# Hybrid retention and RG-LRU layer on one core: half of the retention heads two places later, transpositions four places behind, gate weights loaded a step ahead, S2 in tiles of its own

## The chip, the core and the metric

One core of a Trainium2 chip. The metric is the time of one execution on the device, in microseconds (us). The engines of the core run side by side, each through its own instructions in a fixed order, and wait for each other by semaphores: TensorE (PE, with its weight loads as PEld), VectorE (DVE), ScalarE (ACT), GpSimd (POOL, nearly unused here) and SyncE (SP), which issues nearly all the transfers (DMAs) here.

## What is computed

One decoder layer on 1024 tokens of width 1024: a normalisation, one wide input projection, two token mixers side by side, one output projection with the residual, a final normalisation.

```python
xn = rms_norm(h, norm_in_g)
q, k, v, g_ret, x_lru, g_lru = jnp.split(xn @ w_in, IN_SPLITS, axis=-1)
o_ret = group_norm_heads(chunkwise_retention(rotary(q), rotary(k) * d ** -0.5, v))
y_ret = o_ret * silu(g_ret)                       # 8 heads of 128, chunks of 128 tokens
xc = causal_depthwise_conv(x_lru, conv_w, conv_b)
y_lru = rg_lru(xc, gate_a_w, ..., lru_lambda) * silu(g_lru)   # gates: 8 blocks of 128 x 128
h = h + concat(y_ret, y_lru) @ w_out
return rms_norm(h, norm_out_g)
```

Retention goes chunk by chunk: the scores of a chunk with a decay mask, times v, plus q times a state that each chunk updates; then a group norm per head and the gate.

## The kernel before

All matmuls of the projections are fp32 by three matmuls of rounded parts: `mm3` (L109 to L113; the matmul itself is L112) multiplies high by high, high by low and low by high. `split` (L104 to L107) makes the two parts of an operand: the cast to the high part on ACT (L106), the rest on DVE (L107). Large products are done as seven block products P1 to P7 in place of eight, with sums and differences of blocks as operands (`combine`, L188, on DVE).

The program goes through these stages; the times are those of the profiled execution.
- `v_phase` (6 to 88 us): the projection to v, by P1, P2, P5, P6, P7, P3, P4 in this order. The left operand of P6 is the block difference S2. Its DVE combines and its casts stand in the code behind S1's and S3's, and S2 is written in place over the tiles of block A11 (named xA). `token_rms` loads x once more (tile xt), squares it on ACT (L201) and so gets the row scale, which a matmul with the identity spreads over the partitions (`make_rstd_b`, L219).
- 12 quads XL, GL and G, three for each of four pairs p of LRU blocks (88 to 377 us). `Runner.step` runs the seven products of a quad, with the preparation of the next quad's weights (tile wraw) between them; at each `fill()` one entry of the list `fillers` runs. The quad's `post` appends what remains to that list. For XL this is the convolution (tiles cx, cy, xc; its parts xh and xlo), the gate weights (`gate_w_parts`: load of tile graw and its split into gw), the gates (`lru_gates`: 12 matmuls of xh and xlo by gw for each of two blocks), decay and scan.
- 8 quads for q and k (377 to 500 us): rotation on DVE, then writes to `qk_d` in DRAM, from which the retention loads q and k again.
- the LRU half of the output projection (500 to 663 us): 16 units of 24 matmuls (tiles wo, yt), with the pieces of `Retention` as fillers in between. `Retention(0)` (called a) takes four heads, `Retention(1)` (b) the other four. For each chunk n there are `scores(n)` (L796, and L803 for the transposed k; it also loads chunk n+1's q and k, tile qkc, and v), `state(n)` (L817), `out(n)` (L834, L835, and the group norm into tile yn, L848) and `flip(n)` (four 128 x 128 transposes of yn on PE, L856, times the gate, then a write to `o_d`). A piece is a place in the list, and the units of the projection run some 12 matmuls from one place to the next.
- the retention half of the output projection by seven products (663 to 739 us) and the final normalisation.

Which instruction goes where on an engine is decided by a scheduler from the program's order and its dependencies; within an engine the order is then fixed. SP's queue too is in order: a DMA whose tile is still in use holds up those behind it. Tiles come from pools with a fixed number of buffers (vb 6, vo 10, w4 10, and so on); `big()` takes one of the ten buffers of w4.

Of the kernel before, what the change touches and what calls it, by code (L numbers as in the profile page):

```python
# [16 lines left out]
P = 128  # L17
# [23 lines left out]
def hybrid_layer(  # L41
# [25 lines left out]
    def pool_on(side, name, bufs):  # L67
        return tc.tile_pool(name=name, bufs=bufs, side=side, reuse_waits="tile")
# [117 lines left out]
    def combine(out, a, b, op):  # L186
        for o, x_, y_ in zip(out, a, b):
            dve.tensor_tensor(out=o, in0=x_, in1=y_, op=op)  # L188
# [58 lines left out]


    def v_phase():
        with pool_on("left", "vb", 6) as vb, pool_on("left", "vo", 10) as vo:  # L250
            bw, c, todo = {}, {}, []

            def half():
# [13 lines left out]
            def w_parts(name, src):  # L267
                bw[name] = Parts(slabs)
                for i in range(2):
                    bw[name].put(i, src[i])  # L270
# [60 lines left out]

            combine(b11, b11, b22, ALU.add)
            w_parts("P6", b11)
            s3 = xr["A21"]
            combine(s3, xr["A11"], s3, ALU.subtract)
            s2 = xr["A11"]
            combine(s2, s1, s2, ALU.subtract)
            x_parts("P6", s2)
            sp.dma_start(out=cst_sb, in_=cst)
            sp.dma_start(out=ident, in_=ident_in)  # L340
            todo.extend(token_rms(vb, "bt"))
# [279 lines left out]
    def lru_quads():  # L621
        quads = []
        for p in range(4):
            bs = (2 * p, 2 * p + 1)
            g, gw = {}, []

            def gate_w_parts(p=p, gw=gw):
                gr = sums.tile([P, 2, 512], F32, name="graw", tag="sum")
                sp.dma_start(out=gr[:, 0], in_=gate_w[:, 512 * p:512 * p + 512])
                gw.append(gwp.tile([P, 2, 512], F32R, name="gw", tag="gw"))  # L630
                split(gr[:, 0], gw[0][:, 0], gw[0][:, 1])

            def post_x(q, bs=bs, gw=gw, gate_w_parts=gate_w_parts):
                x0, x1 = lru_conv(bs[0], q.cx), lru_conv(bs[1], q.cy)
                fillers.extend(x0 + [
                    gate_w_parts, x1[0], lambda: lru_gates(gw[0], bs[0]), *x1[1:], None, None,
                    lambda: lru_gates(gw[0], bs[1]), lambda: lru_decay(bs), lambda: lru_root(bs), lambda: lru_scan(bs[0]),
                    lambda: lru_scan(bs[1])])

            def post_g(q, bs=bs, g=g):  # L640
                def gate(b, c):
                    dve.tensor_tensor(out=c, in0=c, in1=rstd_b, op=ALU.mult)
                    act.activation(out=c, in_=c, func=AF.Silu)
                    g[b] = c
                for b, c in zip(bs, (q.cx, q.cy)):
                    fillers.extend([lambda b=b, c=c: gate(b, c), lambda b=b: lru_gated(b, g)])

            quads.append(Quad(C_XL + 256 * p, w4, "w4", post_x))
            quads.append(Quad(C_GL + 256 * p, w4, "w4", post_g))
            quads.append(Quad(C_G + 256 * p, w4, "w4", post_gr(p)))  # L650
        return quads
# [120 lines left out]
    class Retention:  # L772
        def __init__(self, hf):
            self.hf = hf
            self.mask = mask_sb[:, 4 * hf:4 * hf + 4]
            self.st = None
            self.sm, self.qk, self.v, self.kn, self.g = {}, {}, {}, {}, {}

        def load(self, n):
            self.qk[n] = op["qkc"].tile([P, 2, 512], F32, name="qkc", tag="qkc")  # L780
            sp.dma_start(out=self.qk[n],
                         in_=qk_d[self.hf, n].rearrange("p j h c -> p j (h c)"))
            self.v[n] = ph_next["vc"].tile([P, 512], F32, name="vc", tag="vc")
            sp.dma_start(out=self.v[n], in_=v_d[self.hf, n])
            act.activation(out=self.v[n], in_=self.v[n], func=AF.Copy, scale=rstd[:, n:n + 1])
            self.g[n] = ph_next["gch"].tile([P, 512], F32, name="gch", tag="gch")
            sp.dma_start(out=self.g[n], in_=g_d[self.hf, n].rearrange("p h c -> p (h c)"))

        def scores(self, n):
            if n == 0:  # L790
# [35 lines left out]

        def out(self, n):

            hf, q, vn, sm, st = self.hf, self.qk.pop(n)[:, 0], self.v.pop(n), self.sm.pop(n), self.st
            po = psum()  # L830
            for h in range(4):
                hs = slice(h * P, (h + 1) * P)
                if st is not None:
                    pe.matmul(po[:, hs], q[:, hs], st[:, h], start=True, stop=False)  # L834
                pe.matmul(po[:, hs], sm[:, h], vn[:, hs], start=st is None, stop=True)  # L835
            stats = small.tile([P, 4, 6], F32, name="stats", tag="stats")
            mv = small.tile([P, 4, 2], F32, name="mv", tag="mv")
            heads(lambda h, hs: dve.bn_stats(out=stats[:, h], in_=po[:, hs]))
            heads(lambda h, hs: dve.bn_aggr(out=mv[:, h], in_=stats[:, h]))
            ve = small.tile([P, 4], F32, name="ve", tag="ve")  # L840
            dve.tensor_tensor(out=ve, in0=mv[:, :, 1], in1=cst_sb[:, H + 4 * hf:H + 4 * hf + 4],
                              op=ALU.add)
            rs = rsqrt_act(ve, 4)
            yn = ph_next["yn"].tile([P, 512], F32, name="yn", tag="yn")
            nb = small.tile([P, 4], F32, name="nb", tag="nb")
            dve.scalar_tensor_tensor(out=nb, in0=mv[:, :, 0], scalar=-1.0, in1=rs, op0=ALU.mult,  # L846
                                     op1=ALU.mult)
            heads(lambda h, hs: act.activation(out=yn[:, hs], in_=po[:, hs], func=AF.Identity,  # L848
                                               scale=rs[:, h:h + 1], bias=nb[:, h:h + 1]))
            self.yn = yn  # L850
            self.st = self.st_next

        def flip(self, n):

            py, yn = psum(), self.yn
            heads(lambda h, hs: pe.transpose(py[:, hs], yn[:, hs], ident))  # L856
            ot = ph_next["ot"].tile([P, 512], F32, name="ot", tag="ot")
            dve.tensor_tensor(out=ot, in0=py, in1=self.g.pop(n), op=ALU.mult)
            sp.dma_start(out=o_d[self.hf, :, :, n * P:(n + 1) * P].rearrange("h p c -> p h c"),
                         in_=ot.rearrange("p (h c) -> p h c", h=4))  # L860

    def pieces(a, b):

        def first(r, n):
            if n < NT:
                r.scores(n)
            if n:
                r.flip(n - 1)

        f = []  # L870
        for n in range(NT + 1):
            m = n - 1
            f.append(lambda n=n: first(a, n))
            if m >= 0:
                f.append(lambda m=m: first(b, m))
            if n < NT:
                f.append(lambda n=n: (a.state(n), a.out(n)))
            if m >= 0:
                f.append(lambda m=m: (b.state(m), b.out(m)))
        return f + [None, lambda: first(b, NT)]  # L880

    p_a, p_b, *rest = pieces(Retention(0), Retention(1))
    rest[0], rest[1] = rest[1], rest[0]
    fillers.extend([None, None, p_a, None, p_b] + rest)

    wt, ys, xop = {}, {}, {}

# [37 lines left out]
    for dh in range(2):  # L925
        cols = slice(dh * HALF, (dh + 1) * HALF)
        w_cur = w_o
        for t in range(NT):
            if dh == 0 and 0 < t < NT - 1:
                load_yl(t + 1)  # L930
            if dh == 0 and t == 2:
                w_o = group(D, HALF, (0,))
            ps = psum()
            unit_o(ps, yl[t], w_cur, slice(0, HALF), (3, 7) if dh == 0 else (2, 5, 7))
            r = hres[t][:, cols]
            with tc.issue_after(last_load[0].ins):
                sp.dma_start(out=r, in_=x[t * P:(t + 1) * P, cols])
            dve.tensor_tensor(out=r, in0=ps, in1=r, op=ALU.add)
            if dh == 0 and t == NT - 2:
                w_o += group(D, HALF, (2, 4, 6))  # L940
            if dh == 1 and t == 2:
                w_load("11", "wraw", 0, 0)
                w_parts("P1", "11")
            if dh == 1 and t == 4:
                w_load("21", "wraw", 1, 0)
                w_parts("P2", "21")
            if dh == 1 and t == 5:
                y_block(0, 0)
                y_parts("P1", ys[0, 0])
            if dh == 1 and t == 6:  # L950
                y_block(1, 0)
                w_load("11", "wraw", 0, 0)
# [196 lines left out]
```

## Time and profile before

| | |
|---|---|
| median of three runs | 748.6 us (748.37 to 748.61) |
| the profiled execution | 748.8 us |
| its span, first to last instruction | 747.0 us |
| PE busy | 724.4 us, 97% |
| DVE busy | 582.7 us, 78% |
| ACT busy | 425.5 us, 57% |
| mean granted clock of TensorE | 0.993 |

The profiled execution's time is 1.8 us longer than its span. PE is the busiest engine by far, so time is to be sought in the stretches where PE stands still or runs at a lower clock; the busy shares of the other engines are means over stages with different limits.

### The profile page before, as it was taken

What the parts mean: (1) busy time and instruction counts of PE and PEld (TensorE: products, weight loads), DVE (VectorE), ACT (ScalarE), POOL (GpSimd) and SP (SyncE); (2) the same over time, 40 slices, a digit from 0 to 9 for tenths busy, and PEclk for the clock granted to TensorE, in tenths of its full rate; (3) what the DMA queues carried; (4) which work ended last, traced back from release to release, by engine and by line L of the source; (5) the groups of instructions that cost most, each with busy time, mean ns of one, the idle gap of its engine ahead of it and who ended that gap; (6) DMA issues with size and microseconds to landing.
All of it is one profiled execution on the core that took longest, in us unless ns stands there. A gap on an engine that the chain in (4) does not pass through costs nothing.

```text
span 747.0 us, 9358 instructions
## 1 busy us (share of the span) xinstructions
PE 724.4 (97%) x3448; PEld 601.7 (81%) x3448; DVE 582.7 (78%) x960; ACT 425.5 (57%) x649; POOL 0.2 (0%) x4
## 2 busy tenths in 40 slices
PE   6999999999999999999999999997999999999995
PEld 5877888887788788878788888886989988888884
DVE  6899647678977977996799988686467565779996
ACT  6795435695689679669833333244444445424545
POOL 0000000000000000000000000000000000000000
PEclk9999999999999999999999999999899999999998
DMA  9862712122213410421644444569897776272006
GB/s 308 279 207 86 254 56 72 57 84 85 70 57 105 135 57 32 142 97 54 197 126 128 114 113 113 141 187 286 273 312 255 253 210 211 72 228 81 1 0 226
DMA packets 93806, 107.68 MB, mean 144 GB/s; under 512 B 4928, under 2 KB 66752, under 8 KB 93760
## 3 DMA queue, kind: packets, MB, share of 16 engines
q1 hardware_dynamic: 93616, 106.82, 45.5%
q8 instruction: 27, 0.44, 0.2%
q10 hardware_dynamic: 144, 0.26, 0.1%
q14 instruction: 19, 0.16, 0.1%
HBM read 77.71 MB, written 29.36 MB: 143 GB/s over the span
## 4 chain that ended last, share of the span: by engine, by line
PE 55%; DVE 22%; ACT 11%; DMA 7%; issue 4%; SPq 0%; DVEq 0%; ACTq 0%
PE pp L112 47%; DVE xc L561 2%; DVE h L1003 2%; PE pp L796 2%; PE pp L835 2%; PE pp L834 2%; DVE wt L107 2%; PE pp L817 1%; DVE wq L107 1%; DVE y L614 1%; PE pp L856 1%; ACT wq L106 1%; DVE blk L188 1%; DMA rot<-in_rot_t 1%; DMA blk<-o_d 1%
## 5 line engine op out<-in xcount | busy, mean ns | idle before, releaser
L112 PE MATMUL pp<-wh,wq 128*128 128x512 f32 x960 | 301.5, 390 | 1.6 <-DVE cy L471 0.7
L112 PEld LDWEIGHTS pp<-wh,wq 128*128 128x128 f32 x960 | 179.9, 188 | 42.5 <-ACT cy L461 2.3
L112 PE MATMUL pp<-wl,wq 128*128 128x512 f32 x480 | 186.9, 389 | 0.0
L112 PEld LDWEIGHTS pp<-wl,wq 128*128 128x128 f32 x480 | 90.1, 188 | 18.6
L112 PE MATMUL pp<-wo,yt 128*128 128x512 f32 x384 | 98.4, 403 | 0.0
L112 PEld LDWEIGHTS pp<-wo,yt 128*128 128x128 f32 x384 | 70.7, 191 | 13.1
L107 DVE TENSOR_TENSOR wq<-t,wq 128x1024 fp32r<-128x1024 f32 x40 | 48.6, 1220 | 38.6 <-ACT wq L106 31.5
L106 ACT CAST wq<-t 128x1024 fp32r<-128x1024 f32 x40 | 41.7, 1051 | 31.7 <-PE pp L112 22.0
L112 PE MATMUL pp<-wh,w 128*128 128x512 f32 x160 | 52.9, 391 | 0.1
L112 PE MATMUL pp<-wh 128*128 128x512 f32 x112 | 45.5, 406 | 6.9 <-ACT wh L106 6.9
L112 PE MATMUL pp<-wl,wh 128*128 128x512 f32 x112 | 44.6, 400 | 0.0
L112 PE MATMUL pp<-wh,wl 128*128 128x512 f32 x112 | 44.2, 399 | 0.0
L112 PEld LDWEIGHTS pp<-wh,w 128*128 128x128 f32 x160 | 30.0, 188 | 6.9 <-DVE w L107 0.6
L461 ACT COPY cy<-pp 128x512 f32<-128x512 f32 x20 | 11.6, 581 | 41.9 <-PE pp L112 41.3
L848 ACT ACTIVATE yn<-pp,nb,rs_y 128x128 f32<-128x128 f32 x64 | 24.1, 457 | 17.2 <-DVE nb L846 17.2
L112 PEld LDWEIGHTS pp<-wh 128*128 128x128 f32 x112 | 21.7, 194 | 12.1 <-ACT wh L106 7.3
L112 PE MATMUL pp<-wl,w 128*128 128x512 f32 x80 | 31.1, 389 | 0.0
L112 PE MATMUL pp<-wt,ylh 128*128 128x512 f32 x96 | 29.6, 389 | 0.0
L112 PE MATMUL pp<-wt,qkch 128*128 128x512 f32 x96 | 29.6, 389 | 0.0
L422 ACT CAST wq<-wraw 128x512 fp32r<-128x512 f32 x40 | 22.9, 617 | 9.0 <-PE pp L112 8.2
L106 ACT CAST wt<-blk 128x1024 fp32r<-128x1024 f32 x14 | 14.6, 1050 | 21.5 <-PE pp L112 18.0
L424 DVE TENSOR_TENSOR wq<-wraw,wq 128x512 fp32r<-128x512 f32 x40 | 26.8, 681 | 0.1
(179 smaller groups left out, 1303.7 us busy)
## 6 DMA issues: line engine op xcount, KB each, us to landing
wraw<-in_w_in SPq DMA_DIRECT2D x40, 512.0 KB, 4.8
qkc<-qk_d SPq DMA_DIRECT2D x16, 512.0 KB, 6.3
blk<-in_w_out SPq DMA_DIRECT2D x12, 512.0 KB, 5.5
bt<-in_w_in SPq DMA_DIRECT2D x20, 256.0 KB, 5.4
xA<-in_xT SPq DMA_DIRECT2D x16, 256.0 KB, 5.4
v_d<-vo SPq DMA_DIRECT2D x16, 256.0 KB, 2.3
xt<-in_x SPq DMA_DIRECT2D x8, 512.0 KB, 3.3
l_d<-y SPq DMA_DIRECT2D x8, 512.0 KB, 3.0
```

Of the source, the lines that this page charges most:

```text
L106: act.copy(out=hi, in_=src)
L107: dve.tensor_tensor(out=lo, in0=src, in1=hi.bitcast(F32), op=ALU.subtract)
L112: pe.matmul(ps, a, b, start=first and j == 0, stop=last and j == 2, skip_group_check=True)
L422: act.copy(out=h[:, j], in_=b)
L424: dve.tensor_tensor(out=l[:, j], in0=b, in1=h[:, j].bitcast(F32), op=ALU.subtract)
L461: act.copy(out=self.cy[:, :TH], in_=self.A)
L561: dve.scalar_tensor_tensor(out=xc[:, d:], in0=c[:, :T - d], scalar=cw[3 - d], in1=xc[:, d:], op0=ALU.mult, op1=ALU.add)
L796: heads(lambda h, hs: pe.matmul(psc[:, hs], k[:, hs], q[:, hs], start=True, stop=True))
L834: pe.matmul(po[:, hs], q[:, hs], st[:, h], start=True, stop=False)
L835: pe.matmul(po[:, hs], sm[:, h], vn[:, hs], start=st is None, stop=True)
L848: heads(lambda h, hs: act.activation(out=yn[:, hs], in_=po[:, hs], func=AF.Identity, scale=rs[:, h:h + 1], bias=nb[:, h:h + 1]))
L1003: last_add[0] = dve.tensor_tensor(out=r, in0=r, in1=ps, op=op_)
```

## The change

Four parts.
- In `v_phase` S2 gets two tiles of its own (named xS2), and its combine and its parts stand ahead of S3's combine. The pool vb gets a buffer more, vo two less.
- The load of the gate weights moves from the filler `gate_w_parts` to the start of `post_x`, into a buffer of w4 (named gr); the split stays a filler.
- In the retention `flip(n-1)` moves from beside `scores(n)` to just ahead of `state(n)` and `out(n)` of the same half of the heads, four places after its own `out`; b's pieces begin two places later, and the swap of two places at the start is gone. The gate values (tile gch) are loaded in `out`, not in `load`.
- In the units t = 6 and 7 of the first column half there are three places for fillers, not two.

```diff
-        with pool_on("left", "vb", 6) as vb, pool_on("left", "vo", 10) as vo:
+        with pool_on("left", "vb", 7) as vb, pool_on("left", "vo", 8) as vo:
...
             w_parts("P6", b11)
+            s2 = [vb.tile([P, 2, 512], F32, name="xS2", tag="bt") for _ in range(2)]
+            combine(s2, s1, xr["A11"], ALU.subtract)
+            x_parts("P6", s2)
             s3 = xr["A21"]
             combine(s3, xr["A11"], s3, ALU.subtract)
-            s2 = xr["A11"]
-            combine(s2, s1, s2, ALU.subtract)
-            x_parts("P6", s2)
...
-            def gate_w_parts(p=p, gw=gw):
-                gr = sums.tile([P, 2, 512], F32, name="graw", tag="sum")
-                sp.dma_start(out=gr[:, 0], in_=gate_w[:, 512 * p:512 * p + 512])
+            def gate_w_load(p=p, gw=gw):
+                gw.append(big(name="gr"))
+                sp.dma_start(out=gw[0][:, :512], in_=gate_w[:, 512 * p:512 * p + 512])
+
+            def gate_w_parts(gw=gw):
+                gr = gw.pop()
                 gw.append(gwp.tile([P, 2, 512], F32R, name="gw", tag="gw"))
-                split(gr[:, 0], gw[0][:, 0], gw[0][:, 1])
-
-            def post_x(q, bs=bs, gw=gw, gate_w_parts=gate_w_parts):
+                split(gr[:, :512], gw[0][:, 0], gw[0][:, 1])
+
+            def post_x(q, bs=bs, gw=gw, gate_w_load=gate_w_load, gate_w_parts=gate_w_parts):
+                gate_w_load()
...
-            self.g[n] = ph_next["gch"].tile([P, 512], F32, name="gch", tag="gch")
-            sp.dma_start(out=self.g[n], in_=g_d[self.hf, n].rearrange("p h c -> p (h c)"))
...
         def out(self, n):
 
+            self.g[n] = ph_next["gch"].tile([P, 512], F32, name="gch", tag="gch")
+            sp.dma_start(out=self.g[n], in_=g_d[self.hf, n].rearrange("p h c -> p (h c)"))
...
-        def first(r, n):
-            if n < NT:
-                r.scores(n)
+        def second(r, n):
             if n:
                 r.flip(n - 1)
+            if n < NT:
+                r.state(n)
+                r.out(n)
 
         f = []
         for n in range(NT + 1):
             m = n - 1
-            f.append(lambda n=n: first(a, n))
+            if n < NT:
+                f.append(lambda n=n: a.scores(n))
             if m >= 0:
-                f.append(lambda m=m: first(b, m))
-            if n < NT:
-                f.append(lambda n=n: (a.state(n), a.out(n)))
+                f.append(lambda m=m: b.scores(m))
+            f.append(lambda n=n: second(a, n))
             if m >= 0:
-                f.append(lambda m=m: (b.state(m), b.out(m)))
-        return f + [None, lambda: first(b, NT)]
+                f.append(lambda m=m: second(b, m))
+        return f + [None, lambda: second(b, NT)]
 
     p_a, p_b, *rest = pieces(Retention(0), Retention(1))
-    rest[0], rest[1] = rest[1], rest[0]
-    fillers.extend([None, None, p_a, None, p_b] + rest)
+    fillers.extend([None, None, p_a, None, p_b, None] + rest)
...
-            unit_o(ps, yl[t], w_cur, slice(0, HALF), (3, 7) if dh == 0 else (2, 5, 7))
+            unit_o(ps, yl[t], w_cur, slice(0, HALF), (3, 7) if dh == 0 and t < 6 else (2, 5, 7))
```

ACT's order in `v_phase`, around the casts for P6, before (xS_291 and 292 are S1, bt the weights, xA_129 and 130 hold S2; L201 is the square):

```order
28 L201 ACTIVATE xt,ss<-xt 128x1024
29 L106 CAST wh<-bt 128x1024
30 L201 ACTIVATE xt,ss<-xt 128x1024
31 L106 CAST wh<-bt 128x1024
32 L106 CAST wh<-xA_249 128x1024
33 L201 ACTIVATE xt,ss<-xt 128x1024 x2
34 L106 CAST wh<-xA_129 128x1024
35 L201 ACTIVATE xt,ss<-xt 128x1024
36 L106 CAST wh<-xA_130 128x1024
```

And of the change (xS_425 and 426 hold S2):

```order
28 L106 CAST wh<-bt 128x1024 x2
29 L106 CAST wh<-xS_425 128x1024
30 L106 CAST wh<-xS_426 128x1024
31 L201 ACTIVATE xt,ss<-xt 128x1024
32 L106 CAST wh<-xA_249 128x1024
```

The two casts of S2 stood behind four and five squares; they now stand ahead of all of them.

PE's order at the start of the retention, before: the first `out` of a (L817, L835), then the first `scores` of b (L796), then those of a's chunk 1:

```order
1577 L112 MATMUL pp<-wo,yt 128x512 x36
1578 L817 MATMUL pp<-vc,kn 128x128 x2
1579 L835 MATMUL pp<-vc,sm 128x128
1580 L817 MATMUL pp<-vc,kn 128x128 x2
1581 L835 MATMUL pp<-vc,sm 128x128 x3
1582 L796 MATMUL pp<-qkc 128x128 x4
1583 L803 MATMUL pp<-ident,qkc 128x128 x4
1584 L112 MATMUL pp<-wo,yt 128x512 x12
1585 L796 MATMUL pp<-qkc 128x128 x4
1586 L803 MATMUL pp<-ident,qkc 128x128 x4
1587 L856 MATMUL pp<-ident,yn 128x128 x4
```

And of the change, where the first L798 is a's chunk 1 and the second is b's chunk 0:

```order
1584 L839 MATMUL pp<-vc,sm 128x128 x3
1585 L112 MATMUL pp<-wo,yt 128x512 x12
1586 L798 MATMUL pp<-qkc 128x128 x4
1587 L805 MATMUL pp<-ident,qkc 128x128 x4
1588 L112 MATMUL pp<-wo,yt 128x512 x12
1589 L798 MATMUL pp<-qkc 128x128 x4
1590 L805 MATMUL pp<-ident,qkc 128x128 x4
1591 L112 MATMUL pp<-wo,yt 128x512 x12
1592 L860 MATMUL pp<-ident,yn 128x128 x4
```

Two runs of 12 matmuls of 128x512 and the scores of a's chunk 1 now stand between a's first `out` and b's first `scores`; the transposes of yn come 12 matmuls later than before.

SP's queue at the same place, before, from the last write to `qk_d` on (qkc_4039 is b's chunk 0; qkc_3926, a's chunk 1, was loaded earlier):

```order
129 L682 DMA qk_d_75<-cy_3616 64x8x128
130 L784 DMA vc_4041<-v_d_74 128x512
131 L784 DMA vc_4048<-v_d_74 128x512
132 L937 DMA h_3794<-in_x 128x512
133 L787 DMA gch_3924<-g_d_76 128x512
134 L787 DMA gch_3931<-g_d_76 128x512
135 L781 DMA qkc_4039<-qk_d_75 128x1024
136 L787 DMA gch_4044<-g_d_76 128x512
```

And of the change, where qkc_4094 is b's chunk 0 and qkc_4060 is a's chunk 2:

```order
128 L686 DMA qk_d_75<-cy_3618 64x8x128
129 L941 DMA h_3796<-in_x 128x512
130 L728 DMA yraw_4041<-l_d_78 128x8x128
131 L832 DMA gch_3994<-g_d_76 128x512
132 L785 DMA qkc_4060<-qk_d_75 128x1024
133 L788 DMA vc_4062<-v_d_74 128x512
134 L785 DMA qkc_4094<-qk_d_75 128x1024
135 L788 DMA vc_4096<-v_d_74 128x512
```

Ahead of b's load there were five transfers of 256 KB; there are now three of 256 KB and two of 512 KB.

## Rows read from the trace of the kernel before

**Rows 1.** The page: each engine's busy time; the granted clock in 40 slices

```profile
PE 724.4 (97%) x3448; PEld 601.7 (81%) x3448; DVE 582.7 (78%) x960; ACT 425.5 (57%) x649; POOL 0.2 (0%) x4
PEclk9999999999999999999999999999899999999998
```

**Rows 2.** Waits of PE, whole span: total us, times, longest

```profile
PE pp L796 <- DMA qkc<-qk_d: 4.0, 1, 4.0
PE pp L112 <- ACT gw L106: 1.9, 3, 1.0
```

**Rows 3.** Waits of PE's weight loads, whole span

```profile
PEld pp L112 <- ACT gw L106: 3.4, 4, 1.4
PEld pp L856 <- ACT yn L848: 2.4, 9, 0.4
```

**Rows 4.** Timeline of PE, 36 to 46 us: start, duration, instruction [idle before]

```profile
41.81 0.39 PE L112 MATMUL pp<-wh,wl 128*128 128x512 f32 x1
42.88 0.50 PE L112 MATMUL pp<-wh 128*128 128x512 f32 x1 [0.68 <-ACT wh L106]
```

**Rows 5.** Timeline of ACT, same stretch

```profile
40.74 1.06 ACT L201 ACTIVATE xt<-xt 128x1024 f32<-128x1024 f32 x1 [0.48 <-DMA xt<-in_x]
...
41.80 1.03 ACT L106 CAST wh<-xA 128x1024 fp32r<-128x1024 f32 x1
```

**Rows 6.** Timeline of DVE, same stretch

```profile
33.55 2.35 DVE L188 TENSOR_TENSOR bt<-bt 128x1024 f32<-128x1024 f32 x2
35.82 1.22 DVE L188 TENSOR_TENSOR xA<-xA,xA 128x1024 f32<-128x1024 f32 x1
```

**Rows 7.** The tile graw: its instructions, who waited, landing

```profile
L107 DVE TENSOR_TENSOR gw<-graw,gw x4: 681/682/693, 128.3 to 322.9; 128x512 fp32r<-128x512 f32 x4
...
DMA to landing us min/median/max: 3.0/3.1/4.7
```

**Rows 8.** Timeline of PE, 195.3 to 198.2 us

```profile
197.39 0.50 PE L112 MATMUL pp<-xh,gw 128*128 128x512 f32 x1 [1.02 <-ACT gw L106]
```

**Rows 9.** Timeline of DVE, 186 to 199 us

```profile
189.02 1.23 DVE L107 TENSOR_TENSOR xlo<-xc,xh 128x1024 fp32r<-128x1024 f32 x1
```

**Rows 10.** Timeline of PE, 503 to 532 us

```profile
507.35 1.05 PE L796 MATMUL pp<-qkc 128*128 128x128 f32 x8
...
508.59 8.46 PE L112 MATMUL pp<-wo,yt 128*128 128x512 f32 x36
...
518.00 0.83 PE L835 MATMUL pp<-vc,sm 128*128 128x128 f32 x6
522.80 2.08 PE L796 MATMUL pp<-qkc 128*128 128x128 f32 x8 [3.97 <-DMA qkc<-qk_d]
...
529.34 1.06 PE L796 MATMUL pp<-qkc 128*128 128x128 f32 x8
...
530.67 0.60 PE L856 MATMUL pp<-ident,yn 128*128 128x128 f32 x4
531.02 1.16 PE L112 MATMUL pp<-wo,yt 128*128 128x512 f32 x4
```

**Rows 11.** Timeline of SP's queue, 507 to 523 us

```profile
516.30 0.38 SPq L781 DMA_DIRECT2D qkc<-qk_d  x1
```

**Rows 12.** Windows: busy time of each engine, granted clock, DMA share, GB/s

```profile
507.70:518.50 10.80, 10.80 (x62) 9.35 (x61) 7.10 (x8) 4.90 (x9) 0.00 (x0) 1.00 0.91 233
518.50:522.80 4.30, 0.33 (x3) 0.14 (x2) 2.48 (x14) 2.49 (x4) 0.00 (x0) 0.78 0.98 368
522.80:527.70 4.90, 4.90 (x18) 4.41 (x19) 0.76 (x2) 1.93 (x7) 0.00 (x0) 0.50 1.08 362
```

**Rows 13.** The tile qkc, SP's three loads issued 516.3 to 518.9 us

```profile
DMA to landing us min/median/max: 6.5/7.6/8.9
```

**Rows 14.** Timeline of PE, 602 to 606 us

```profile
603.48 1.37 PE L856 MATMUL pp<-ident,yn 128*128 128x128 f32 x4 [0.18 <-ACT yn L848]
604.61 1.64 PE L112 MATMUL pp<-wo,yt 128*128 128x512 f32 x6
```

More of the change, by code (lines that the diff above doesn't have):

```diff
@@ L776, in __init__ @@
             self.st = None
-            self.sm, self.qk, self.v, self.kn, self.g = {}, {}, {}, {}, {}
+            self.sm, self.qk, self.v, self.kn, self.g, self.yn = {}, {}, {}, {}, {}, {}
         def load(self, n):
@@ L849, in out @@
                                                scale=rs[:, h:h + 1], bias=nb[:, h:h + 1]))
-            self.yn = yn
+            self.yn[n] = yn
             self.st = self.st_next
         def flip(self, n):
-            py, yn = psum(), self.yn
+            py, yn = psum(), self.yn.pop(n)
             heads(lambda h, hs: pe.transpose(py[:, hs], yn[:, hs], ident))
```

## Prediction

> **What bounds the kernel now.** I read the page first. PE is busy 724.4 us, 97% of a span of 747.0 us, and the granted clock is full except in the first slices, in one slice past the middle and in the last [rows 1]. So the kernel is bound by PE nearly everywhere, and an edit can only win where PE stands still, or runs at the lower clock. DVE and ACT, at 78% and 57%, matter only where PE waits for them.
>
> Next come the waits of PE. After the start-up the largest one is 4.0 us, once, in L796 (the scores) for the DMA of qkc; then 1.9 us, three times, for the ACT cast of the gate weights, gw [rows 2]. Small matmuls with a wait show in part on the side of the weight loads: there gw is 3.4 us in 4 waits, and L856 (the transposes of yn) waits 2.4 us in 9 for ACT's yn [rows 3]. To these belongs one wait in `v_phase`: the timeline of PE has a matmul at 41.81 and the next at 42.88, released by an ACT cast [rows 4]. The four parts of the change touch just these four places.
>
> **S2 ahead of S3.** In the run of 36 matmuls at 508.59 one takes 8.46 / 36 = 0.23 us [rows 10]. P6's first matmul came 42.88 - 41.81 = 1.07 us after the one before it, so 0.84 us were lost [rows 4]. Its releaser is the cast of S2 (here over xA), 41.80 to 42.83 on ACT; that cast stood behind a square of xt, 40.74 to 41.80, which itself had waited 0.48 us for its DMA [rows 5]. In the new order the cast stands ahead of the first square, and S2's combine follows the two combines of bt on DVE, which now end about 35.9 (two of them took from 33.55 to 35.82, so DVE steps at 1.14 us) [rows 6]. Walking DVE's new order from 35.82: S2's first half, two low parts of bt, S2's second half, its first low part, one combine of S3, its second low part: seven steps, 35.82 + 7 x 1.14 = 43.8. PE, starting P6 at 42.04, wants the last of these at its 12th matmul, 42.04 + 11 x 0.23 = 44.6. So the 0.84 us go, with 0.8 us to spare; bounds 0 (something else is late by as much) and 0.84. The squares go later, hidden by P6, P7 and P3; the row scale that comes from them is wanted only by the matmuls of L219, which move from P3 into P4. By the same walk the scale is ready some 0.7 us ahead of them, so this is where a little could be lost.
>
> **Gate weights.** Before, the load was issued when its filler ran, and landed 3.0 to 4.7 us later [rows 7]; the gates wanted it before that. The worst case is at 197.39 us: PE had been idle 1.02 us for the cast of gw [rows 8]. I take the loss between what PE's side shows (1.9) and what the weight loads show (3.4) [rows 2, 3]: 2.4 us, since a stopped start also stretches the next matmul (0.50 against 0.39 us is the row's own duration) [rows 8]. The added cost is none in instructions: the same four loads, casts and subtractions (0.68 us each on DVE [rows 7]) only sit earlier. But with the weights there the scheduler also puts the gates' first 12 matmuls earlier: for p = 1 by 23 matmuls, 23 x 0.23 = 5.3 us. Then PE wants xlo, the low part of the convolution, at about 197.39 - 1.2 - 5.3 = 190.9. DVE finished xlo at 189.02 + 1.23 = 190.25 [rows 9], and gw's low part, now right behind it, at some 190.9, wanted two matmuls later, 191.4. So it fits with half a microsecond. For p = 2 and 3 the move is 20 and 13 matmuls and the same sum has more room. Bounds: a gain of 3.4, and a loss of about 1.0 if xlo were late at three places by what gw was late by. I take +2.4. The buffer of w4 that the load now holds for most of a quad's steps is one of ten; if it holds up a convolution tile, the cost is again one such wait per quad.
>
> **The first scores of b.** This is the largest term. PE ended a's `out` at 518.00 + 0.83 = 518.83 and got b's first scores at 522.80: 3.97 us idle, as the row says [rows 10]. The clock then fell: in 518.5 to 522.8 the mean granted clock is 0.78, in 522.8 to 527.7 it is 0.50, the 1.2 GHz level [rows 12]. From 522.80 to 529.34 PE did one set of scores and 12 matmuls; at full clock a set takes 508.59 - 507.35 = 1.24 us and the 12 matmuls 2.8, so 6.54 - 4.04 = 2.5 us went to the clock [rows 10]. The two together are 6.5 us.
>
> In the new order two runs of 12 matmuls and a's second scores come first, whose operands were loaded long before: 2.8 + 1.24 + 2.8 = 6.8 us of work. PE then wants b's q and k at 518.83 + 6.8 = 525.6. When do they land? The load can be issued no earlier than the last write to `qk_d` has landed; before, that was at 516.30, and it landed at 522.8 [rows 11, 13]. The new queue has 0.5 MB more ahead of it. At 368 GB/s, the rate in that stretch, this is 1.4 us more; at 233, the lowest rate near it, 2.2 us [rows 12]. So it lands between 524.2 and 525.0, 0.6 to 1.4 us in time. And the longest of the three loads issued there took 8.9 us: 516.3 + 8.9 = 525.2 [rows 13], also in time. I take the whole 6.5 us.
>
> What is late next: the loads behind it. Before, the transfers were saturated up to 530 us (0.91 to 1.08 of the DMA engines in the windows [rows 12]). The next scores come only 2.8 us of matmuls and a state and `out` later, and there are two chunks of slack in the four buffers of qkc.
>
> **Transposes four places behind.** At 603.48 four transposes waited head by head for ACT's yn, and took 604.61 - 603.48 = 1.13 us where four unhindered ones take 531.02 - 530.67 = 0.35 [rows 10, 14]. The weight loads' sum of such waits is 2.4 us [rows 3]. With about two places more between `out` and `flip`, each some 12 matmuls, that is 5 us more for a chain that was late by about 1 us; all go but the last of b, which has no four places left. I take 2.0, bounds 0.2 (the one idle that PE itself shows at 603 [rows 14]) and 2.4. The later load of the gate values (in `out`) still has four places, over 10 us, against 3 to 9 us of landing [rows 7, 13].
>
> The third filler place in two units changes when pieces run, not what runs: 0.
>
> **Sum.** 0.84 + 2.4 + 6.5 + 2.0 = 11.7 us. From the profiled execution's 748.8 this gives 737.1; that execution was 0.2 above the median, so 736.9. I say 737.0.
>
> **Rivals.**
> (a) *b's scores still wait.* Three loads issued one behind another took 6.5 up to 8.9 us [rows 13]: each has to wait for what was issued ahead. If the 0.5 MB ahead costs more than the 1.4 to 2.2 us, say 3 to 5, PE waits up to 2 us, and if the clock falls again another 2.5 come: 737.5 to 741.5. For: the stretch is saturated. Against: even the longest row lands in time. The Trainium skill, "DMA: Bandwidth & Descriptors", section "Queues, rings and completion order", says that on each DMA engine descriptors are consumed in ring order; by it everything issued ahead counts in full and nothing issued behind, which speaks for this rival rather than for a landing at 522.8 as before. The rising landings agree. 18%.
> (b) *The early places are not won.* xlo or the scale of L219 is late where gw was, or DVE, nearly without a pause there, passes the shift on late. Then 1 to 3.2 us of the first two terms stay: 738 to 740.2. For: margins of half a microsecond. Against: the walks above. 17%.
> (c) *The waits only move.* The qkc wait goes to the next load and the transposes wait for the gate values instead. Then only the first two terms are left: about 745.5. Against: the four buffers. 4%.
> (d) *Slower.* The load of the gate values now stands in `out`, and its buffer (gch has three) comes free only after a transposition that is four places late. SP's queue is in order, so each of some 14 such loads can hold the loads of q, k and v behind it. From 12 / 14 = 0.9 us of PE wait per chunk on, nothing is left of the gain; at 1.2 us the time is 748.8 - 11.7 + 14 x 1.2 = 753.9. For: the order of the queue. Against: those loads land in 9 us at most [rows 13], and the list gives each a round of four places, over 10 us. 4%.
>
> **How the numbers follow.** The forecast, with 735.5 to 738.5 as its own range, has 57%. A measurement of this kernel tells changes over 0.2%, 1.5 us. All of the forecast, (a), (b) and most of (c) lie beyond that: faster 0.92, same 0.03, slower 0.05. The range goes from 735.2, where the gates give 3.4 and the transposes 2.4 with a little from the others, up to 743, past (a) and (b); (c) and (d) are left out.
>
> **What the profile would show.** Right: no gap ahead of P6 at 42 us; no wait for gw in the list; no wait for qkc, no slice with a lower clock between start and end, the stretch from a's first `out` to b's first scores filled with 24 matmuls; at most one wait of transposes for yn, near 650. Wrong: a wait for xlo or gw where the gates now stand, a PE wait for L219, a wait in the scores with a clock of 0.5 behind it, or an SP queue that stands at L832.

## The result and the profile after

The changed kernel takes 736.16 us (median of four runs, 735.47 to 736.82) against 748.49 us before: a ratio of 0.984, 95% interval 0.982 to 0.987. Twelve microseconds are gone; 737.0 was forecast. The profiled execution took 735.47 us with a span of 733.7.

The waits of PE over the whole span, as in [rows 2]:

```profile
PE pp L112 <- ACT wh L106: 6.2, 1, 6.2
PE pp L860 <- ACT yn L852: 1.3, 1, 1.3
PE pp L112 <- DVE cy L471: 0.8, 1, 0.8
PE pp L112 <- ACT cy L461: 0.5, 1, 0.5
PE pp L112 <- DVE wq L107: 0.3, 1, 0.3
```

The DMA of qkc and the cast of gw are out of the list; the wait for wh is the start-up alone. One row has grown: yn now costs a single wait of 1.3 us, where PE's side showed 0.2 us before [rows 14].

The timeline of PE ahead of P6 answers [rows 4], with no gap:

```profile
40.43 0.39 PE L112 MATMUL pp<-wh,wl 128*128 128x512 f32 x1
40.66 0.39 PE L112 MATMUL pp<-wh 128*128 128x512 f32 x1
```

P6 starts here at 40.66, 0.23 us after the matmul before it. The timeline from a's first `out` on answers [rows 10]; L839 ends the `out`, the first L798 is a's chunk 1, the second is b's chunk 0:

```profile
512.24 0.83 PE L839 MATMUL pp<-vc,sm 128*128 128x128 f32 x6
512.83 3.00 PE L112 MATMUL pp<-wo,yt 128*128 128x512 f32 x12
515.66 1.05 PE L798 MATMUL pp<-qkc 128*128 128x128 f32 x8
516.55 0.60 PE L805 MATMUL pp<-ident,qkc 128*128 128x128 f32 x4
516.91 3.02 PE L112 MATMUL pp<-wo,yt 128*128 128x512 f32 x12
519.76 1.05 PE L798 MATMUL pp<-qkc 128*128 128x128 f32 x8
```

The stretch is filled, and the windows, whose last three columns are clock, DMA share and GB/s as in [rows 12], keep the clock at 1.00 while the transfers stay as saturated as before:

```profile
515.00:519.00 4.00, 4.00 (x25) 3.53 (x24) 2.47 (x8) 3.10 (x7) 0.00 (x0) 1.00 1.03 406
519.00:530.00 11.00, 11.00 (x72) 9.74 (x71) 6.01 (x17) 5.74 (x13) 0.00 (x0) 1.00 1.01 308
```

The grown wait is b's last transposition. PE's timeline there:

```profile
639.11 3.68 PE L112 MATMUL pp<-wo,yt 128*128 128x512 f32 x15
644.06 0.33 PE L860 MATMUL pp<-ident,yn 128*128 128x128 f32 x1 [1.27 <-ACT yn L852]
```

Fifteen matmuls stand between `out` and the transposes. In the kernel before it was 25, and there was no wait:

```profile
655.14 5.93 PE L112 MATMUL pp<-wo,yt 128*128 128x512 f32 x25
661.04 0.33 PE L856 MATMUL pp<-ident,yn 128*128 128x128 f32 x1
```

What goes into the time that yn needs is on DVE and ACT of the changed kernel. DVE first:

```profile
639.17 1.23 DVE L107 TENSOR_TENSOR qkcl<-blk,qkch 128x1024 fp32r<-128x1024 f32 x1 [0.87 <-PE pp L838]
640.31 0.88 DVE L842 BATCH_NORM_STATS2 stats<-pp 128x6 f32<-128x128 f32 x4
```

and ACT:

```profile
642.60 1.04 ACT L106 CAST ylh<-blk 128x1024 fp32r<-128x1024 f32 x1 [0.69 <-PE pp L112]
643.55 1.50 ACT L852 ACTIVATE yn<-pp,nb,rs_y 128x128 f32<-128x128 f32 x4
```

A split for the last stage stands ahead of the group norm on DVE (1.1 us), a cast for it ahead of yn on ACT (0.95 us). That alone does not explain the wait, since in the kernel before the same split stood in the same place and yn came later still:

```profile
655.20 1.22 DVE L107 TENSOR_TENSOR qkcl<-blk,qkch 128x1024 fp32r<-128x1024 f32 x1 [1.57 <-PE pp L834]
660.53 1.51 ACT L848 ACTIVATE yn<-pp,nb,rs_y 128x128 f32<-128x128 f32 x4 [1.33 <-DVE nb L846]
```

From the first matmul behind `out` to the first yn it took 5.4 us before (655.14 to 660.53) and 4.4 us now (639.11 to 643.55). So what is new is the distance: 15 matmuls are done in 3.7 us, 25 took 5.9.

To see where the time came from, the span is cut at five events of PE's timeline: the first matmul, the last before P6, the first that reads tile wq (12 matmuls into the first quad), the first scores, the first of the last stage (tile wt). The last column ends with PE's last matmul. In microseconds:

| kernel | start to P6 | P6 to quads | quads to scores | scores to last stage | last stage |
|---|---|---|---|---|---|
| before | 35.61 | 49.57 | 415.96 | 155.37 | 76.54 |
| changed | 34.27 | 48.33 | 412.83 | 148.45 | 76.52 |
| changed, second profile | 34.97 | 49.58 | 412.07 | 148.45 | 76.52 |
| S2 undone | 35.23 | 50.95 | 412.32 | 148.44 | 76.52 |
| gates undone | 34.42 | 49.01 | 416.19 | 148.44 | 76.52 |
| b early | 35.23 | 49.67 | 412.91 | 151.95 | 76.52 |
| b early, PE kept busy | 35.60 | 48.59 | 412.61 | 151.09 | 76.52 |
| b one place later | 34.73 | 48.57 | 413.03 | 148.62 | 76.52 |
| flips undone | 34.34 | 48.89 | 412.58 | 153.16 | 76.52 |
| before + b late alone | 34.67 | 52.42 | 415.24 | 150.48 | 76.53 |
| last flip later | 35.63 | 49.56 | 412.67 | 147.14 | 76.52 |
| last flip later, second profile | 35.42 | 48.71 | 412.81 | 147.12 | 76.52 |
| fills undone | 35.56 | 48.90 | 412.89 | 147.03 | 76.57 |
| vb of eight | 34.93 | 48.21 | 412.58 | 147.12 | 76.52 |

In the first column PE has the same matmuls in every kernel, and it still spreads over 1.4 us: they begin to run at the full rate (0.23 us from one to the next) at 9.57 us in the changed kernel's profile, at 12.53 in that of before and at 13.71 in another. Kernels with the same start lie at both ends of the spread, so the 1.3 us that this column gives to the 13.3 between the two profiled spans are taken as chance. The same goes for the stretch behind PE's last matmul, which the table leaves out: 7.7 us before, 7.1 changed, 6.9 to 7.9 over the profiles. Stages are compared below, beside the medians.

### The profile page after: what moved, and what is told of

It is laid out like the page before. It is cut to its first block, busy times and chain, and to the rows that moved or that the text cites. A ratio compares the mean times of both kernels' runs of the same rounds, so it can differ in the third digit from the quotient of the medians.

```text
span 733.7 us, 9359 instructions
## 1 busy us (share of the span) xinstructions
PE 717.3 (98%) x3448; PEld 598.8 (82%) x3448; DVE 582.8 (79%) x960; ACT 425.5 (58%) x649; POOL 0.2 (0%) x4
## 4 chain that ended last, share of the span: by engine, by line
PE 85%; ACT 7%; DVE 4%; DMA 2%; issue 2%; DVEq 0%; SPq 0%
PE pp L112 75%; PE pp L798 2%; PE pp L839 2%; PE pp L838 2%; PE pp L819 2%; PE pp L860 1%; DMA rot<-in_rot_t 1%; PE pp L805 1%; ACT wq L106 1%; DVE y L614 1%; ACT L601 1%; ACT a L601 0%; DMA g_d<-cx 0%; ACT r L602 0%; DMA xA<-in_xT 0%
## 5 line engine op out<-in xcount | busy, mean ns | idle before, releaser
L106 ACT CAST wq<-t 128x1024 fp32r<-128x1024 f32 x40 | 41.6, 1050 | 32.3 <-PE pp L112 26.5
```

Of the source, the lines that this page charges most:

```text
L106: act.copy(out=hi, in_=src)
```

## The experiments

All kernels but one are the changed one with an edit; the exception, b late alone, is the one before.

**b early.** Both places taken back, the rest left.

```diff
-    fillers.extend([None, None, p_a, None, p_b, None] + rest)
+    rest[0], rest[1] = rest[1], rest[0]
+    fillers.extend([None, None, p_a, None, p_b] + rest)
```

> The changed kernel (736.2 us) with b's first scores where they were, right behind a's first out; all other parts stay. My account: the wait for b's q and k (4.0 us) and the half clock behind it (2.5 us) come back, so about 742.7 us, with a PE wait of 3.5 to 4.5 us in the scores and a clock of 0.5 in the 5 us after it. Rival (the place matters little, the stretch was slow because the transfers are saturated there): the wait stays below 1.5 us and the time under 738.

740.94 us, ratio 0.990 (0.988 to 0.992). PE's timeline:

```profile
514.48 0.83 PE L839 MATMUL pp<-vc,sm 128*128 128x128 f32 x6
518.63 2.07 PE L798 MATMUL pp<-qkc 128*128 128x128 f32 x8 [3.32 <-DMA qkc<-qk_d]
520.49 1.06 PE L805 MATMUL pp<-ident,qkc 128*128 128x128 f32 x4
521.21 3.17 PE L112 MATMUL pp<-wo,yt 128*128 128x512 f32 x12
524.21 1.05 PE L798 MATMUL pp<-qkc 128*128 128x128 f32 x8
```

and the windows behind the wait:

```profile
518.50:520.00 1.50, 1.37 (x6) 1.37 (x7) 0.00 (x0) 0.00 (x0) 0.00 (x0) 0.50 1.19 341
520.00:521.50 1.50, 1.50 (x9) 1.50 (x8) 0.76 (x2) 0.00 (x0) 0.00 (x0) 0.50 1.03 368
521.50:523.00 1.50, 1.50 (x8) 1.24 (x7) 0.67 (x5) 1.41 (x6) 0.00 (x0) 0.99 1.05 393
```

Wait and clock are back, a little smaller than in the kernel before: 3.3 us instead of 4.0, and the clock rises after three microseconds, not five. From 518.63 to 524.21 the work of 4.1 us took 5.58, so the clock cost 1.5 us here. The rival is out. The 742.7 us that I expected were 1.8 too many. The two costs are 1.7 us smaller than the 6.5 that I took over, and the stage grew by 3.5 us rather than their 4.8, because the wait of 1.3 us for yn at b's last transposition is not in this kernel's list; the median grew by 4.8 us, so the other 1.3 lie outside the stage.

How much clock is lost differs from one execution to the next. The mean granted clock on record is 0.992 in three of the six runs (740.87 to 742.26 us), 0.996 in the profiled one, and 0.998 and 0.999 in the two fastest (738.67 and 738.92 us); the changed kernel's eight runs have 0.997 or 0.998. So, by the means, two executions lost next to nothing and three lost more than the profile shows. That all of it lies behind this wait is likely but not shown, since only one run was profiled.

**b early, PE kept busy.** As above, with 18 matmuls that nobody reads between a's `out` and b's scores.

```diff
+    def busy():
+        ps, t = psum(), max(yl)
+        for _ in range(18):
+            pe.matmul(ps, yl[t][0][:, 0], w_o[0][0][:, :HALF], start=True, stop=True,
+                      skip_group_check=True)
...
+    fillers.extend([None, None, p_a, None, lambda: (p_b(), busy())] + rest)
```

> b's first scores early as in the run b_early, but 18 matmuls of 128x512 whose result nobody reads (an extra, the output is unchanged) stand between a's first out and b's first scores, 4.1 us of work in the place of the idle time. My account (the lower clock came from the idle time): the clock stays full, the scores and 12 matmuls behind it take 4.0 us instead of 6.5, and the run is 2.5 us faster than b_early although it does more. Rival (the slow 5 us come from the saturated transfers): no faster than b_early, and the scores as slow as there.

739.05 us, 1.9 below b early; by the ratios to the kernel before, 0.988 (0.987 to 0.990) against 0.990 (0.988 to 0.992), the two overlap, so the stage has to decide. PE's timeline, where L893 are the extra matmuls:

```profile
514.22 4.36 PE L893 MATMUL pp<-wo,yt 128*128 128x512 f32 x18
518.42 1.05 PE L798 MATMUL pp<-qkc 128*128 128x128 f32 x8
519.31 0.60 PE L805 MATMUL pp<-ident,qkc 128*128 128x128 f32 x4
519.67 3.02 PE L112 MATMUL pp<-wo,yt 128*128 128x512 f32 x12
522.52 1.05 PE L798 MATMUL pp<-qkc 128*128 128x128 f32 x8
```

The windows over the scores and the 12 matmuls behind them, first of b early, then of this run:

```profile
518.60:524.20 5.60, 5.57 (x24) 5.07 (x25) 1.43 (x6) 2.61 (x9) 0.00 (x0) 0.74 1.09 361
518.40:522.50 4.10, 4.10 (x25) 3.58 (x24) 1.13 (x2) 2.78 (x7) 0.00 (x0) 1.00 1.08 370
```

The same work now takes 522.52 - 518.42 = 4.10 us instead of 5.58, at a clock of 1.00 instead of 0.74, while the DMA engines are as busy (1.08 against 1.09, 370 against 361 GB/s). So the slow microseconds behind the wait come from the idle time and not from the transfers. The stage is 0.9 us shorter than b early's, though 18 x 0.23 = 4.1 us of useless work replaced 3.3 us of waiting. The 2.5 us that I expected were the clock cost of the kernel before; b early's profile had only 1.5 to win.

**b one place later.**

```diff
+    rest[0], rest[1] = rest[1], rest[0]
     fillers.extend([None, None, p_a, None, p_b, None] + rest)
```

> The changed kernel with b's first scores one place later than before instead of two: 12 matmuls (2.8 us) between a's first out and b's first scores. My account: the load lands about 4.0 us after a's out, so a wait of 1.0 to 1.5 us is left, and such a wait leaves the clock full as those of about 1 us at 196 us did: 737.2 to 737.7 us. Rival (the clock falls at any wait): 739.7 us or more.

737.38 us, and the stage is 148.62 us against 148.45. The timeline of PE has no gap ahead of the scores:

```profile
513.77 3.00 PE L112 MATMUL pp<-wo,yt 128*128 128x512 f32 x12
516.67 1.16 PE L798 MATMUL pp<-qkc 128*128 128x128 f32 x8
```

Only the weight loads show a wait, 0.3 us. My 1.0 to 1.5 us was wrong, though the median fell into the range that I gave: the load, issued at 511.26, landed after 5.4 us, 2.9 us after a's `out` had made way for the next matmul, not some 4. One place was enough in this profile, with nothing to spare; the median lies 0.7 to 1.2 us above the changed kernel's two, which the 0.2 us of the stage does not explain. With both places the load has more ahead of it: in the changed kernel it was issued at 510.79 and landed after 7.1 us, 5.1 us after a's `out`, and is wanted 6.9 us after it.

**b late alone.** The kernel before with this one edit.

```diff
-    rest[0], rest[1] = rest[1], rest[0]
-    fillers.extend([None, None, p_a, None, p_b] + rest)
+    fillers.extend([None, None, p_a, None, p_b, None] + rest)
```

> The kernel before with one edit alone: b's pieces two places later and the swap gone. My account: the 6.5 us of wait and clock go, 742.0 us; with the last transposition's own wait up to 1.5 us less of a gain. Rival (the gain needs the later gate loads in out as well, since the gate values stand ahead of b's load in the queue here): a wait of 1 us or more is left in the scores, 743 to 746 us.

746.03 us (743.22 to 749.34, twelve runs), ratio 0.998 (0.996 to 1.000): far less than the 6.5 us. No wait for qkc is left, so the rival is out too; the stage is 4.9 us shorter, which fits the 6.5 less the 1.6 us that one transposition on PE's side now waits for yn. On the weight loads' side the waits for yn rose to 3.9 us (2.4 before [rows 3]), 1.9 of it in one. A second loss, which the edit does not touch, sits in `v_phase`: the wait ahead of P6 was 2.27 us in this profile, and the clock fell behind it.

```profile
40.70:43.20 2.50, 0.44 (x2) 0.02 (x1) 2.50 (x3) 2.12 (x5) 0.00 (x0) 1.00 0.53 177
43.20:47.40 4.20, 3.98 (x11) 3.16 (x12) 3.81 (x5) 3.46 (x6) 0.00 (x0) 0.59 0.70 222
```

How many of the other eleven runs had that is not known, since only one was profiled. Their mean granted clocks are on record: 0.999 in the fastest (743.22 us), 0.993 and 0.994 in the three slowest (748.90 to 749.34 us). Those three lost more clock than the profiled run (0.996); where, nothing shows, and so the 1.8 us of the median are not accounted for stage by stage.

**Flips undone.** The transposes stand beside `scores` again.

```diff
+        def first(r, n):
+            if n < NT:
+                r.scores(n)
+            if n:
+                r.flip(n - 1)
...
-        return f + [None, lambda: second(b, NT)]
+        return f + [None, lambda: first(b, NT)]
```

> The changed kernel with the transposes back beside the scores of the same half of the heads; b stays two places later. The forecast gave the later transposes 2.0 us: by it about 738.2 us. The trace of the changed kernel speaks for less: the stage gained only some 0.4 us beside the 6.5 us of the first scores, since the very last transposition now waits 1.3 to 1.7 us. By that about 736.6 us, with waits for yn of some 2 us on the weight loads' side, spread over several transpositions, and that of the last one still there.

740.96 us, 4.3 to 4.8 more than the changed kernel's two medians; both numbers that were expected are too low. The waits of the weight loads:

```profile
PEld pp L860 <- ACT yn L852: 6.6, 15, 1.7
```

Fifteen transpositions wait, where before it was nine for 2.4 us. In this order a `flip` two places behind its `out` is worse off than in the kernel before, presumably because b moved and the places lie closer, which was not tested by itself; so the four places are worth 4.7 us in this order (153.16 against 148.45), but that does not make them worth 4.7 us over the kernel before.

**S2 undone.**

```diff
-        with pool_on("left", "vb", 7) as vb, pool_on("left", "vo", 8) as vo:
+        with pool_on("left", "vb", 6) as vb, pool_on("left", "vo", 10) as vo:
...
-            s2 = [vb.tile([P, 2, 512], F32, name="xS2", tag="bt") for _ in range(2)]
-            combine(s2, s1, xr["A11"], ALU.subtract)
-            x_parts("P6", s2)
             s3 = xr["A21"]
             combine(s3, xr["A11"], s3, ALU.subtract)
+            s2 = xr["A11"]
+            combine(s2, s1, s2, ALU.subtract)
+            x_parts("P6", s2)
```

> The changed kernel with S2 in place over A11 again, behind S3, and the two pools as before. My account: the wait ahead of P6 (0.84 us, and 0.2 us at its ninth matmul) comes back, 737.0 to 737.4 us. Rival (the earlier P6 only moves the wait to the matmuls of the row scale): no difference, 736.2 us, with no wait of TensorE for the row scale in this run where the changed kernel has one.

739.71 us, 3.0 to 3.6 above the changed kernel and over 2 us above what I expected; the rival is out. The wait ahead of P6 is back, and larger than before; PE:

```profile
41.38 0.39 PE L112 MATMUL pp<-wh,wl 128*128 128x512 f32 x1
44.03 0.50 PE L112 MATMUL pp<-wh 128*128 128x512 f32 x1 [2.27 <-ACT wh L106]
```

and ACT, where S2's cast at 42.95 stands behind squares that wait for xt:

```profile
37.36 1.06 ACT L201 ACTIVATE xt<-xt 128x1024 f32<-128x1024 f32 x1 [1.70 <-DMA xt<-in_x]
...
41.90 1.06 ACT L201 ACTIVATE xt<-xt 128x1024 f32<-128x1024 f32 x1 [0.44 <-DMA xt<-in_x]
42.86 0.18 ACT L201 ACTIVATION_READ_ACCUMULATOR xt<-xt 128x1 f32 x1
42.95 1.03 ACT L106 CAST wh<-xA 128x1024 fp32r<-128x1024 f32 x1
```

The cost of the old order hangs on when xt lands, and on when PE gets there (it was ready for P6 at 41.6 us here, at 42.0 before): 0.84 us in the profile of before, 2.4 here, and 2.4 with a lower clock behind it in b late alone. The mean clocks of the six runs go from 0.998 (737.76 us) down to 0.994 (740.46 and 740.47 us), where the changed kernel's eight have 0.997 or 0.998; so some executions of the old order seem to lose clock too, which the profiled one did not.

**Gates undone.** The load is in `gate_w_parts` again.

```diff
+                gr = sums.tile([P, 2, 512], F32, name="graw", tag="sum")
+                sp.dma_start(out=gr[:, 0], in_=gate_w[:, 512 * p:512 * p + 512])
...
-                gate_w_load()
```

> The changed kernel with the gate weights loaded in the filler again, into the old buffer. My account: three waits for gw come back, 1.9 us on TensorE's side and 3.4 us with the weight loads; 738.6 to 739.3 us. Rival (the load's time matters little, the gates waited for the convolution's parts just as long): under 737 us, with a wait for xlo or gw in the changed kernel too.

739.8 us, half a microsecond above the range that I gave, and the quads take 416.19 us against 412.83. The waits are there again, on the side of PE and of its weight loads:

```profile
PE pp L112 <- ACT gw L106: 2.2, 3, 1.4
PEld pp L112 <- ACT gw L106: 3.8, 4, 1.8
```

The stage's 3.4 us lie near the row of the weight loads and not that of the matmuls. The rival is out.

**Last flip later.** One more empty place ahead of b's last transposition; measured twice, the second time together with the changed kernel itself.

```diff
-        return f + [None, lambda: second(b, NT)]
+        return f + [None, None, lambda: second(b, NT)]
```

> The changed kernel with one more empty place ahead of b's last transposition, so that it stands 24 matmuls of 128x512 behind its out instead of 15. My account: the 1.3 to 1.7 us that it waits for yn go, 734.5 to 734.9 us. Rival (the last transposition now comes too late for the loads of the last stage): a wait of TensorE near the start of the last stage takes back what was won, 736 us or more.

> The run last_flip once more, beside the changed kernel in one call. If the 1.3 us that its retention stage was shorter are real: that stage again 147.1 us, and the median 1 to 1.5 us below the changed kernel's. If the median is level again, something else in this kernel takes back what was won.

> The changed kernel once more, as it is, so that small differences stand against its own spread in this call. By its first runs 736.2 us, the stage from the first scores to the last stage 148.45 us as in its first profile, and in the start-up a clock that rises anywhere between 9.5 and 13 us.

PE's timeline of the second:

```profile
640.20 5.73 PE L112 MATMUL pp<-wo,yt 128*128 128x512 f32 x24
645.77 0.76 PE L860 MATMUL pp<-ident,yn 128*128 128x128 f32 x4
```

The wait is gone and the stage is 1.3 us shorter in both profiles, with nothing lost in the last stage. The medians say less: 736.12 us the first time, 735.65 the second against 736.68 for the changed kernel measured with it, where the intervals of the ratios (0.981 to 0.985 and 0.983 to 0.986) overlap.

**Fills undone.**

```diff
-            unit_o(ps, yl[t], w_cur, slice(0, HALF), (3, 7) if dh == 0 and t < 6 else (2, 5, 7))
+            unit_o(ps, yl[t], w_cur, slice(0, HALF), (3, 7) if dh == 0 else (2, 5, 7))
```

> The changed kernel with two places for fillers in units 6 and 7 of the first half again. If these two places are what pulls the last transposition of b ahead by 15 matmuls, it now stands near the end of the stage and does not wait for yn: retention stage near 147.1 us, 735 us in all; the late write to o_d would then show as a wait in the last stage, up to 1 us, if its loads are short of time. If the places are worth nothing either way, as the forecast had it: 736.2 us with the wait of 1.3 us still there.

735.16 us; the stage is 147.03 us, the wait for yn of 1.3 us is gone, and the last stage is 76.57 instead of 76.52. Twenty matmuls stand ahead of the first transposition here, which is enough. So the two added places are what pulled the last transposition ahead, and they cost 1.4 us.

**vb of eight.** The run last flip later with

```diff
-        with pool_on("left", "vb", 7) as vb, pool_on("left", "vo", 8) as vo:
+        with pool_on("left", "vb", 8) as vb, pool_on("left", "vo", 6) as vo:
```

It was made for a wait that the profile of the changed kernel does not have but its second profile does:

```profile
65.50 0.50 PE L112 MATMUL pp<-wh,wl 128*128 128x512 f32 x1 [0.64 <-DVE wl L107]
```

ACT's timeline in that profile shows a cast behind a square that waits for its DMA again, 18 us further on:

```profile
59.52 1.06 ACT L201 ACTIVATE xt<-xt 128x1024 f32<-128x1024 f32 x1 [0.88 <-DMA xt<-in_x]
60.49 0.18 ACT L201 ACTIVATION_READ_ACCUMULATOR xt<-xt 128x1 f32 x1
60.58 1.03 ACT L106 CAST wh<-bt 128x1024 fp32r<-128x1024 f32 x1
```

> The run last_flip with one more buffer for the pool of bt, xt and S2 (eight), and two less for the results of v (six). If the wait of 0.8 us near 65 us, which some executions of the kernels with S2 in its own tiles show, comes from the squares of xt that were pushed later by the fewer buffers, it is gone in this profile and the median is 0.3 to 0.8 us below last_flip_again. If the six result buffers are too few, a wait for a v_d write appears in P7, P3 or P4 and the run is slower.

734.78 us, ratio 0.983 (0.981 to 0.984), the lowest median of all, and the row is not in its profile; its casts of bt start at 58.36 and 60.26. But it is not in the first profile of the changed kernel either, and 735.65 for last flip later lies within the spread. Whether the eighth buffer helps stays open; that it costs nothing is all the runs show. It, last flip later and fills undone are the versions that I would keep, with no claim on their order.

## Why the prediction was right, point by point

The forecast was 737.0 us by a sum of 11.7; the result is 12.3 less than before by the medians. The largest term held, three others were off by one to two microseconds each, and that their errors partly cancelled is luck.

- **The first scores of b, 6.5 us: right.** Against the stage without any of these waits (147.1 us in last flip later) the kernel before lost 155.37 - 147.13 = 8.2 us, of which 4.0 were the wait [rows 2] and 2.5 the clock, worked out from [rows 10]. All of the 6.5 is gone. That the clock belongs to the idle time was shown by the busy run; its size of 2.5 us is that of one execution, as b early's runs show. The load landed 5.1 us after a's `out` in the changed order, against 4.2 before (the weight loads' own wait there); the 0.9 us more lie under the 1.4 to 2.2 that I gave the 0.5 MB, so rival (a) never came near. The Trainium skill, "DMA: Bandwidth & Descriptors", section "Queues, rings and completion order", has each DMA engine consume its descriptors in ring order; the trace agrees in direction, since the same load landed after 5.4 us with less issued ahead of it and after 7.1 us with more. Of the 0.9 us, 0.6 are a longer way from issue to landing (7.1 against 6.5 us [rows 13]) and the rest is an issue nearer to `out`; how much of the 0.6 the extra data made was not tested.
- **The transposes, 2.0 us: the term that was mis-sized, at the step "all go but the last of b".** 8.2 - 6.5 = 1.7 us were lost to them before. The changed kernel wins that and pays 1.3 us for b's last transposition (148.45 against 147.1). Net 0.4. I took its distance from the list, as two places still; in PE's order it went from 25 matmuls behind its `out` to 15, and yn, which takes 4.4 us to start, is not ready after the 3.7 us of those. Elsewhere the distance grew by more than was said: by the two orders shown, a's first transposes stand 36 matmuls behind their `out` where it was 12, so 24 later and not 12.
- **The third filler place, 0 us: wrong.** It brought the last transposition forward; taken back, the stage is 1.4 us shorter. This and the term above are one loss.
- **Gate weights, 2.4 us: right in mechanism, too small.** Undoing them costs 3.4 us in the stage, and the two first profiles differ by 3.1. My upper bound, from the weight loads [rows 3], was the value; I took a figure between. The reordering that came with the early weights did no harm: for p = 1 xlo was ready at 187.45 and gw at 188.04, PE's first matmul with them started at 188.18, and no wait for either is in the list.
- **S2, 0.84 us: right in mechanism, too small, since it is not one number.** The wait was 0.84 us in the profile that I had, and 2.4 in two others of the same order. The pieces from P6 to the quads take 49.6, 51.0 and 52.4 us in the three profiles with the old order and 48.2 to 49.7 in the eleven with the new one; the means are 51.0 and 48.9, so some 2 us, over the 0.84 that was my upper bound; the medians of S2 undone say 3.0 to 3.6. A part is given back in some executions, where the later squares hold up a cast for P3 (0.8 us near 65). "Hidden by P6, P7 and P3" was true in only some.
- **Rivals (b), (c) and (d)** left little: no wait for xlo, for the gate values, or for a later qkc load is in the list, and SP's waits have no row for L832. The matmuls of the row scale, L219, wait 0.8 us for their operand on the side of the weight loads.
- What lifted the profiled difference to 13.3 us beyond these is the start-up with 1.3 us and the stretch behind PE's last matmul with 0.6, both taken as chance.

## What to carry to other kernels

A DMA wait of PE can cost more than its idle time: in two profiles here 3.3 and 4.0 us of it carried 1.5 and 2.5 us of half clock behind them, so work that is ready is worth putting there even for one place, and in one test even useless work shortened the stage, by 0.9 us. An instruction that waits for a DMA on an in-order engine (the squares on ACT) makes everything behind it as random as the transfer; one profile then shows one draw of that cost, not its size. And when a list of pieces is shifted, its last entry has to be followed by itself in the engine's order, counted in matmuls and not in places.

## What was not expected of the hardware

In the same code, with the same idle time ahead of P6 (2.27 us), the clock stayed full in one profile (1.00 in the window from 44 to 48 us, S2 undone) and fell in another (mean 0.59 over the next 4.2 us, b late alone). And the start-up of one and the same code has the full rate from 9.57 us in one execution, 3.4 us after its first matmul, and from 13.71 in another, 6.3 us after it.
